# The MLP's second weight: every operand summed, split and stored during the first product, and one load per item in the second

## The chip, the core and the metric

One core of a Trainium2 chip runs the kernel. The metric is device time in microseconds for one execution, lower is better; the time of a kernel is the median of its runs.

## What is computed

The reference is one layer of a decoder: RMSNorm, an input projection whose columns feed four head groups (gated convolution, two attentions with compressed keys or latents, stick-breaking attention), their norms, an output projection and a residual; then the part that matters here, the MLP on x of 2048 x 1024 with 4096 hidden columns, all in float32:

```python
h2 = rms_norm(x, norm2_w[l])
x = x + jnp.square(jax.nn.relu(h2 @ ffn_w1[l])) @ ffn_w2[l]
```

## The kernel before

**Split operands.** A float32 operand goes through the matmul as two parts, `hi` (a copy rounded to the matmul's type) and `lo` (the operand less `hi`), and a product is three matmuls, hi x hi, hi x lo and lo x hi. `split_s` (L216) makes the parts: ScalarE copies (L219), VectorE or GpSimd subtracts (L220).

**Seven products for eight.** Both MLP products are made of 2 x 2 blocks by a Strassen-like scheme: seven products of sums of quarters, `PARTS` (L1689) naming for each product the quarter of the first and of the second operand. `sums` (L1875) turns the first operand's quarters step by step into the sums, on GpSimd (four per chunk, L1878 to L1883).

**First product** (`items1`, 224 items of 12 matmuls, 128x512 each): per slice f of 256 hidden columns and half of the tokens seven items. `load1` fetches a slice of `ffn_w1` on SP's queue into `yr` or `hr`; `prep1` splits a quarter into a slot of `wslot` (L1846), 11 slots cut from the two big tiles `b0` and `b1` (`parts`, seven pieces of 2048 columns) that the attention has left; preparation runs 7 items ahead. `product1` sums into a PSUM bank (six banks in turn), evacuates it by VectorE, or by ScalarE for product 1 (L1920), and `hidden` (L1900) applies relu and square on ScalarE and stores to `ud` in DRAM from ScalarE's queue (L1907). The other operand lies split in SBUF (`form`).

**Sums of the second weight.** `weight_sums` (L2008) runs beside the first product, one step per item: for each chunk it loads the four quarters of `ffn_w2` into `rawb` (L2012), makes four sums on GpSimd (L2017) and stores them unsplit to `wsd` (L2021), all on SP's queue.

**Second product** (`items2`, two halves of the tokens). The 4096 rows of the second weight go in chunks `CH`: one double (two blocks of 128 rows per quarter), one single, six double, and a last single one without the scheme. A chunk has seven items (four for the last), an item four token tiles, each of 6 (double) or 3 (single) matmuls into one bank; `add` (L2113) adds the bank to an accumulator `accp` by VectorE (L2117), or copies it by ScalarE in a half's first chunk (L2115). The last chunk is `plain2` (L2132), two items to a bank. `combine` (L2150) adds accumulators to each other, half on VectorE and half on GpSimd, after the last chunk of the scheme; `store` (L2154) writes the rows out.

`preps2` prepares items ahead of the product, as many as the ring `ops` has pairs (ten tiles, so five). `prep2` (L2025) splits both operands of an item into the item's pair: the first from `ZA` (loaded by `load_a`, L1992, from `ud`), the second from `ZB` (loaded by `load_bs`, L2005, 512 KB from `ffn_w2` or, for the four sums, from `wsd`, into a ring `rb` of eight). `LOA` and `LOB` name the subtracting engine for each of a chunk's seven items:

```python
split_s(za[ka], oa[:, 0, 0:nm], oa[:, 1, 0:nm], eng=E[LOA[j]])
split_s(ZB.pop(n), ob[:, 0, 0:nm], ob[:, 1, 0:nm], eng=E[LOB[j]])
```

**Order of the work.** The framework orders each engine's instructions when the program is built: program order is the priority, and an instruction goes ahead when its operands are ready and its engine is free in the builder's own timeline. On the chip every engine, and every engine's DMA queue, runs that order and waits at its head. So the weight sums, written one step per item over some 170 items, run in the first part of the product.

Of the kernel before, what the change touches and what calls it, by code (L numbers as in the profile page):

```python
# [20 lines left out]
P = 128  # L21
# [27 lines left out]
LOA, LOB = 'ddddddd', 'pdpdddd'  # L49
# [83 lines left out]
def _build(ctx, nc, tc, a, out, dbg, upto):  # L133
# [1544 lines left out]
    def tail():  # L1678
# [17 lines left out]
        with ExitStack() as c1:  # L1696
# [131 lines left out]
            for i in range(NT):  # L1828
# [7 lines left out]
                if i:  # L1836
# [10 lines left out]
                     for (t, c) in [(parts[q], 2) for q in (3, 2, 0, 1, 6)] + [(b0[:, 8192:9216], 1)] for n in range(c)]  # L1847
# [115 lines left out]
            def op2(t):  # L1963
                return t.rearrange("p (s m n) -> p s m n", s=2, m=2)

            ops = [op2(parts[q]) for q in (0, 1, 6, 3, 2)] + [None] + [op2(parts[q]) for q in (4, 5)] + [None, None]
            NOP = len(ops)


            ra, rb = [], []  # L1970
            ZA, ZB = {}, {}
            done2, loaded_b = [0], [0]

            wsd = {(c, p): dram.tile([P, ch[1], 512], F32, name="wsd%d_%d" % (c, p))
                   for c, ch in enumerate(CH) if ch[2] for p in (4, 5, 6, 7)}
# [18 lines left out]
            def load_bs(upto):  # L1994
                while loaded_b[0] < min(upto, len(items2)):
                    k = loaded_b[0]
                    h, c, j = items2[k]
                    nm, inside = CH[c][1:]
                    z = ZB[k] = blocks(rb[k % 8], nm)
                    p = ORDER2[j]  # L2000
                    if inside and p > 3:
                        src = wsd[c, p]
                    else:
                        src = quarter(c, PARTS[p][1] if inside else PLAIN[j][1])
                    Q[W2Q].dma_start(z, src)  # L2005
                    loaded_b[0] += 1

            def weight_sums(c):  # L2008
                nm = CH[c][1]
# [5 lines left out]
                for (n, o, x, y, op, p) in ((0, 22, 22, 12, ALU.subtract, 7), (1, 12, 12, 11, ALU.subtract, 5),  # L2015
                                            (2, 11, 22, 11, ALU.add, 6), (3, 21, 21, 11, ALU.subtract, 4)):
                    E[SUB[n]].tensor_tensor(z[o], z[x], z[y], op)  # L2017
                    yield
                    yield
                for (q, p) in ((22, 7), (12, 5), (11, 6), (21, 4)):  # L2020
                    Q[W2Q].dma_start(wsd[c, p], z[q])  # L2021
                    yield
                    yield
# [77 lines left out]
            with ExitStack() as c2:  # L2101
                wr = c2.enter_context(tc.tile_pool(name="fr", bufs=1, side="right", reuse_waits="tile"))
                wp = c2.enter_context(tc.tile_pool(name="fw", bufs=1, reuse_waits="tile"))
                for n in (5, 8, 9):
                    ops[n] = wr.tile([P, 2, 2, 512], F32R, name="op2_%d" % n)
# [105 lines left out]
```

## Time and profile before

| | us |
|---|---|
| median of three runs | 3069.57 |
| the runs | 3068.2 to 3080.05 |
| the profiled execution | 3078.75 |
| its span (first to last instruction) | 3077.0 |

| engine | busy | share of the span |
|---|---|---|
| TensorE | 2914.2 | 95% |
| VectorE | 2265.1 | 74% |
| ScalarE | 1647.7 | 54% |
| GpSimd | 1337.6 | 43% |

The first product of the MLP begins near 1785 us of the span, the second at 2407.6. The engine names in the rows below: PE is TensorE (PEld its weight loads), DVE VectorE, ACT ScalarE, POOL GpSimd, SP SyncE, and a q behind one is its queue. A row of a timeline has the start, the duration, the engine, the line, the operation, the tiles (written <- read), the form and the count, and in brackets the idle time before it and what ended that.

### The profile page before, as it was taken

To read this page: it belongs to the slowest core of one execution; us is meant where nothing else is said; L and a number is where in the kernel's file an instruction comes from. 1 tells how busy PE (TensorE), PEld (TensorE's weight loads), DVE (VectorE), ACT (ScalarE), POOL (GpSimd) and SP (SyncE) were. 2 spreads that over 40 slices of the span, in tenths; PEclk is the share of its full clock that TensorE was granted. 3 is DMA by queue.
4 is the path that set the end of the run, shared out by engine and by line. 5 is a ranking of instruction groups with operands and counts; after the bars stand their busy time and mean duration, and the time that the engine had idled before them with its cause. 6 is when DMAs were issued, how large, how long until landed. Compare 5 with 4: busy or idle time off the path is not lost. (4 is left out here: it accounts for less than half of the span.)

```text
span 3077.0 us, 43654 instructions
## 1 busy us (share of the span) xinstructions
PE 2914.2 (95%) x14111; PEld 2324.2 (76%) x14123; DVE 2265.1 (74%) x4782; ACT 1647.7 (54%) x3328; POOL 1337.6 (43%) x1311
## 2 busy tenths in 40 slices
PE   7999999899888999999989989999999999989998
PEld 7867898687666667766668868887888777877887
DVE  7843357798777787777678676766444699999998
ACT  5622334677686768787855344456555533334331
POOL 1210102455565667676522267635222343364334
PEclk9999999899888999999999999999999999999999
DMA  8556643522320110010034569745333644364431
GB/s 243 161 137 210 195 146 112 144 81 61 102 83 21 28 37 21 27 41 15 28 118 145 187 209 322 279 144 175 110 109 110 233 151 150 117 215 157 151 127 72
DMA packets 311752, 398.18 MB, mean 129 GB/s; under 512 B 67167, under 2 KB 206091, under 8 KB 311267
## 3 DMA queue, kind: packets, MB, share of 16 engines
q1 hardware_dynamic: 279635, 351.73, 36.1%
q10 hardware_dynamic: 31344, 41.82, 3.7%
q8 instruction: 112, 1.84, 0.2%
q0 software_dynamic: 544, 1.84, 0.2%
q14 instruction: 117, 0.96, 0.1%
HBM read 262.64 MB, written 132.69 MB: 128 GB/s over the span
## 5 line engine op out<-in xcount | busy, mean ns | idle before, releaser
L971 POOL TENSOR_TENSOR pw<-pf,ph 128x512 fp32r<-128x512 f32 (+2 forms) x264 | 326.3, 1248 | 145.3 <-ACT pf L968 101.9
L139 PE MATMUL ptr<-form,big 128*128 128x512 f32 x1152 | 281.0, 393 | 8.6 <-ACT ft L1920 4.5
L139 PE MATMUL pmm<-form,big 128*128 128x512 f32 x1152 | 278.6, 391 | 2.3 <-ACT big L219 1.9
L139 PEld LDWEIGHTS ptr<-form,big 128*128 128x128 f32 x1152 | 216.9, 189 | 57.5 <-ACT ft L1920 5.4
L963 ACT ACTIVATE ph<-pmm 128x512 fp32r<-128x512 f32 (+2 forms) x366 | 210.5, 575 | 93.0 <-PE pmm L139 71.4
L139 PEld LDWEIGHTS pmm<-form,big 128*128 128x128 f32 x1152 | 216.0, 188 | 49.7 <-ACT big L219 2.3
L139 PE MATMUL pmm<-big 128*128 128x512 f32 (+5 forms) x816 | 218.6, 394 | 6.2 <-DVE accp L2117 5.2
L139 PE MATMUL pmm<-whl,hth 128*128 128x256 f32 (+2 forms) x1024 | 218.4, 304 | 4.1 <-ACT hth L219 3.6
L1306 POOL TENSOR_TENSOR sg<-sg,ce 128x512 f32<-128x512 f32 (+3 forms) x160 | 155.6, 974 | 144.3 <-DVE ce L1304 116.8
L219 ACT ACTIVATE big<-raw 128x1024 fp32r<-128x1024 f32 (+2 forms) x116 | 100.8, 882 | 178.2 <-PE ptr L139 97.9
L220 DVE TENSOR_TENSOR big<-hr,big 128x512 fp32r<-128x512 f32 (+1 forms) x125 | 141.6, 1135 | 64.5 <-ACT big L219 64.1
L139 PE MATMUL pmm<-big,big 128*128 128x512 f32 (+5 forms) x672 | 178.7, 393 | 10.6 <-DVE accp L2117 10.0
L139 PEld LDWEIGHTS pmm<-big 128*128 128x128 f32 (+2 forms) x816 | 154.3, 192 | 42.2 <-ACT op L219 5.7
L139 PE MATMUL ptr<-big 128*128 128x512 f32 (+2 forms) x645 | 178.9, 400 | 4.3 <-DVE mx L1208 1.7
L139 PE MATMUL pmm<-big,ar 128*128 128x512 f32 x736 | 182.3, 397 | 0.0
L139 PEld LDWEIGHTS pmm<-whl,hth 128*128 128x128 f32 x1024 | 169.8, 195 | 10.6 <-issue 4.6
L220 DVE TENSOR_TENSOR big<-yr,big 128x512 fp32r<-128x512 f32 (+1 forms) x125 | 126.2, 1012 | 54.7 <-ACT big L219 53.9
L139 PE MATMUL pmm<-hth,whl 128*128 128x512 f32 x480 | 157.1, 403 | 7.7 <-ACT whl L223 4.5
L139 PEld LDWEIGHTS pmm<-big,ar 128*128 128x128 f32 x736 | 136.7, 189 | 29.0 <-ACT ar L219 0.3
L2117 DVE TENSOR_TENSOR accp<-accp,ptr 128x512 f32<-128x512 f32 x224 | 151.6, 677 | 6.7 <-PE ptr L139 6.4
L139 PEld LDWEIGHTS pmm<-big,big 128*128 128x128 f32 (+2 forms) x672 | 125.1, 190 | 41.1 <-DVE accp L2117 11.9
L2117 DVE TENSOR_TENSOR accp<-accp,pmm 128x512 f32<-128x512 f32 x224 | 151.5, 676 | 6.3 <-PE pmm L139 6.3
(488 smaller groups left out, 7961.6 us busy)
## 6 DMA issues: line engine op xcount, KB each, us to landing
ud<-ft ACTq DMA_DIRECT2D x124, 256.0 KB, 2.0
xt<-x SPq DMA_DIRECT2D x32, 512.0 KB, 6.0
yr<-ffn_w SPq DMA_DIRECT2D x16, 1024.0 KB, 6.0
hr<-ffn_w SPq DMA_DIRECT2D x16, 1024.0 KB, 5.2
rawb<-ffn_w SPq DMA_DIRECT2D x28, 512.0 KB, 4.9
wsd<-rawb SPq DMA_DIRECT2D x28, 512.0 KB, 6.2
rawb<-ud SPq DMA_DIRECT2D x28, 512.0 KB, 3.3
raw<-wsd SPq DMA_DIRECT2D x28, 512.0 KB, 6.2
```

The costliest lines, as they stand in the source:

```text
L139: anchor[0] = pe.matmul(o, l, r, start=start, stop=stop)
L219: act.activation(hi, src, AF.Copy)
L220: (eng or dve).tensor_tensor(lo, src, hi.bitcast(F32), ALU.subtract)
L963: act.activation(ph[:, 0:n], pl[:, 0:n], AF.Exp)
L971: sub.tensor_tensor(pw[:, 0:n], pf[:, 0:n], ph[:, 0:n].bitcast(F32), ALU.subtract)
L1306: pool.tensor_tensor(sg[:, o:512], sg[:, o:512], ce[:, o + 1:513], ALU.mult)
L2117: dve.tensor_tensor(acc[p][:, t], acc[p][:, t], pt, ALU.add)
```

## The change

The second operand of the second product is prepared whole beside the first product. `weight_forms` takes the place of `weight_sums`: for all nine chunks it loads the four quarters, and for each of the seven operands of a chunk (the last chunk: its four quarters) `two_parts` splits it (ScalarE copies, VectorE subtracts) and, a step later, stores both parts to `wsd` from ScalarE's queue. `hi` goes to one of two halves of `parts[6]`; `lo` to the other half where the quarter is still needed for sums, otherwise over the quarter itself. The four sums per chunk stay on GpSimd. In the second product `prep2` splits only the first operand; the second comes as both parts in one load on SP's queue, straight into its place in the ring. `load_bs`, `rb`, `ZB` and `LOB` go; the ring grows from ten tiles to twelve (six items ahead) and takes its pieces of the big tiles in another order; `wslot` has nine slots, since `parts[6]` is now the staging.

```diff
-                     for (t, c) in [(parts[q], 2) for q in (3, 2, 0, 1, 6)] + [(b0[:, 8192:9216], 1)] for n in range(c)]
+                     for (t, c) in [(parts[q], 2) for q in (3, 2, 0, 1)] + [(b0[:, 8192:9216], 1)] for n in range(c)]
...
-            ops = [op2(parts[q]) for q in (0, 1, 6, 3, 2)] + [None] + [op2(parts[q]) for q in (4, 5)] + [None, None]
+            ops = [op2(parts[q]) for q in (3, 6, 0, 2, 1)] + [None] + [op2(parts[q]) for q in (4, 5)] + [None] * 4
...
-            wsd = {(c, p): dram.tile([P, ch[1], 512], F32, name="wsd%d_%d" % (c, p))
-                   for c, ch in enumerate(CH) if ch[2] for p in (4, 5, 6, 7)}
+            wsd = {(c, p): dram.tile([P, 2, ch[1], 512], F32, name="wsd%d_%d" % (c, p))
+                   for c, ch in enumerate(CH) for p in (range(1, 8) if ch[2] else (11, 12, 21, 22))}
+            stage = [parts[6][:, n * 1024:(n + 1) * 1024] for n in range(2)]
+            staged_n = [0]
...
-            def weight_sums(c):
-                nm = CH[c][1]
+            def weight_forms(c):
+                nm, inside = CH[c][1:]
                 z = {q: blocks(ra[n], nm) for n, q in enumerate((22, 12, 11, 21))}
                 for q in z:
                     Q[W2Q].dma_start(z[q], quarter(c, q))
                 for _ in range(5):
                     yield
...
+                def two_parts(q, p, keep):
+                    staged_n[0] += 1
+                    hi = blocks(stage[staged_n[0] % 2], nm)
+                    lo = blocks(stage[(staged_n[0] + 1) % 2], nm) if keep else z[q].bitcast(F32R)
+                    split_s(z[q], hi, lo)
+                    yield
+                    act.dma_start(wsd[c, p][:, 0], hi.bitcast(F32))
+                    act.dma_start(wsd[c, p][:, 1], lo.bitcast(F32))
...
+                if inside:
+                    yield from two_parts(22, 3, True)
+                    add(0, 22, 22, 12, ALU.subtract)
+                    yield
+                    yield
+                    yield from two_parts(11, 1, True)
+                    add(1, 12, 12, 11, ALU.subtract)
+                    add(2, 11, 22, 11, ALU.add)
+                    yield
+                    yield
+                    yield from two_parts(21, 2, True)
+                    add(3, 21, 21, 11, ALU.subtract)
                     yield
                     yield
                 for (q, p) in ((22, 7), (12, 5), (11, 6), (21, 4)):
-                    Q[W2Q].dma_start(wsd[c, p], z[q])
-                    yield
+                    yield from two_parts(q, p if inside else q, False)
                     yield
...
-                split_s(ZB.pop(n), ob[:, 0, 0:nm], ob[:, 1, 0:nm], eng=E[LOB[j]])
+                Q[W2Q].dma_start(ob[:, :, 0:nm].bitcast(F32), wsd[c, p if inside else kb])
...
-                    load_bs(min(done2[0] + 8, len(rb) if len(rb) < 8 else len(items2)))
...
-            wsums = iter([g for c, ch in enumerate(CH) if ch[2] for g in [weight_sums(c)]])
+            wsums = iter([weight_forms(c) for c in range(len(CH))])
...
-                    load_bs(4)
...
-                for n in (5, 8, 9):
+                for n in (5, 8, 9, 10, 11):
```

## Rows read from the trace of the kernel before

**Rows 1.** The page, part 1: busy us, share of the span, instructions.

```profile
PE 2914.2 (95%) x14111; PEld 2324.2 (76%) x14123; DVE 2265.1 (74%) x4782; ACT 1647.7 (54%) x3328; POOL 1337.6 (43%) x1311
```

**Rows 2.** Stretches: length, then PE, PEld, DVE, ACT, POOL busy; clock, DMA, GB/s.

```profile
1785.00:2413.00 628.00, 614.86 (x2664) 501.54 (x2665) 374.81 (x463) 327.70 (x545) 293.23 (x183) 0.99 0.52 181
1830.00:1980.00 150.00, 149.81 (x655) 122.66 (x654) 106.29 (x103) 69.75 (x119) 116.64 (x60) 1.00 0.88 312
2413.00:3073.00 660.00, 630.89 (x2690) 508.11 (x2688) 627.06 (x678) 233.10 (x266) 283.96 (x126) 0.98 0.44 152
```

**Rows 3.** Timeline of PE in the second product.

```profile
2407.63 1.52 PE L139 MATMUL pmm<-big 128*128 128x512 f32 x6
...
2452.30 0.84 PE L139 MATMUL pmm<-big 128*128 128x512 f32 x3
...
2460.51 0.87 PE L139 MATMUL pmm<-big,big 128*128 128x512 f32 x3
...
2471.72 1.62 PE L139 MATMUL pmm<-big 128*128 128x512 f32 x3 [2.43 <-DVE accp L2117]
...
2476.92 1.55 PE L139 MATMUL pmm<-op,op 128*128 128x512 f32 x6
...
2548.90 1.52 PE L139 MATMUL pmm<-op,big 128*128 128x512 f32 x6
...
2588.85 1.53 PE L139 MATMUL pmm<-op,op 128*128 128x512 f32 x6
...
2717.97 0.84 PE L139 MATMUL pmm<-op,op 128*128 128x512 f32 x3
...
2733.75 0.86 PE L139 MATMUL pmm<-big 128*128 128x512 f32 x3
...
3050.53 0.84 PE L139 MATMUL pmm<-op,op 128*128 128x512 f32 x3
...
3061.47 0.86 PE L139 MATMUL pmm<-big 128*128 128x512 f32 x3
...
3072.01 0.86 PE L139 MATMUL ptr<-op,big 128*128 128x512 f32 x3
```

**Rows 4.** Waits of PE, 2416 to 3077: us in total, times, longest us.

```profile
PE pmm L139 <- DVE accp L2117: 15.2, 5, 6.7
PE ptr L139 <- DVE accp L2117: 12.5, 10, 2.6
```

**Rows 5.** Timeline of all engines, 2464 to 2468.

```profile
2464.22 2.37 POOL L1879 TENSOR_TENSOR rawb<-rawb,rawb 128x1024 f32<-128x1024 f32 x1
2464.32 3.35 DVE L220 TENSOR_TENSOR big<-rawb,big 128x1024 fp32r<-128x1024 f32 x1
...
```

**Rows 6.** Instructions on two tiles, op and accp: ns min/median/max, first and last start.

```profile
L219 ACT ACTIVATE op<-hr x12: 614/1044/1051, 2400.5 to 3012.4; 128x1024 fp32r<-128x1024 f32 x10, 128x512 fp32r<-128x512 f32 x2
L220 DVE TENSOR_TENSOR op<-raw,op x28: 678/1214/3421, 2422.4 to 3043.8; 128x1024 fp32r<-128x1024 f32 x23, 128x512 fp32r<-128x512 f32 x5
L220 POOL TENSOR_TENSOR op<-raw,op x8: 1293/2408/3400, 2425.5 to 2986.2; 128x1024 fp32r<-128x1024 f32 x6, 128x512 fp32r<-128x512 f32 x2
...
L2117 DVE TENSOR_TENSOR accp<-accp,ptr x224: 672/675/690, 2421.8 to 3072.9; 128x512 f32<-128x512 f32 x112
```

**Rows 7.** A stretch at the start of the second product, columns as in rows 2.

```profile
2410.00:2420.00 10.00, 9.54 (x42) 7.48 (x41) 3.48 (x2) 5.87 (x10) 2.47 (x2) 1.00 1.04 395
```

**Rows 8.** The page, part 6: DMA issues, KB each, median us to landing.

```profile
wsd<-rawb SPq DMA_DIRECT2D x28, 512.0 KB, 6.2
...
accp<-x2d SPq DMA_DIRECT2D x8, 1024.0 KB, 6.5
```

**Rows 9.** Issues on the tile ud from ScalarE's queue: ns min/median/max.

```profile
L1907 ACTq DMA_DIRECT2D ud<-ft x124: 325/326/359, 1824.4 to 2418.1; - x124
```

**Rows 10.** Waits of SP's queue, 1790 to 2413: us in total, times, longest.

```profile
SPq L2021 <- POOL rawb L2017: 63.8, 25, 6.8
SPq L2012 <- DMA wsd<-rawb: 38.6, 16, 4.9
```

More of the change, by code (lines that the diff above doesn't have):

```diff
@@ L48 @@
 SU1, SUA, SUB = 'pppp', 'pppp', 'pppp'
-LOA, LOB = 'ddddddd', 'pdpdddd'
+LOA = 'ddddddd'
 SQE = 'aaaa'
@@ L1964, in op2 @@
                 return t.rearrange("p (s m n) -> p s m n", s=2, m=2)
-            ops = [op2(parts[q]) for q in (0, 1, 6, 3, 2)] + [None] + [op2(parts[q]) for q in (4, 5)] + [None, None]
+            ops = [op2(parts[q]) for q in (3, 6, 0, 2, 1)] + [None] + [op2(parts[q]) for q in (4, 5)] + [None] * 4
             NOP = len(ops)
-            ra, rb = [], []
-            ZA, ZB = {}, {}
-            done2, loaded_b = [0], [0]
-            wsd = {(c, p): dram.tile([P, ch[1], 512], F32, name="wsd%d_%d" % (c, p))
-                   for c, ch in enumerate(CH) if ch[2] for p in (4, 5, 6, 7)}
+            ra, ZA = [], {}
+            done2 = [0]
+            wsd = {(c, p): dram.tile([P, 2, ch[1], 512], F32, name="wsd%d_%d" % (c, p))
+                   for c, ch in enumerate(CH) for p in (range(1, 8) if ch[2] else (11, 12, 21, 22))}
+            stage = [parts[6][:, n * 1024:(n + 1) * 1024] for n in range(2)]
+            staged_n = [0]
             def blocks(t, nm):
@@ L1992, in load_a @@
                 Q[UQ].dma_start(z, src if nm == 2 else src[:, m % 2:m % 2 + 1])
[L1994 to L2006, printed above, removed]
-            def weight_sums(c):
-                nm = CH[c][1]
+            def weight_forms(c):
+                nm, inside = CH[c][1:]
                 z = {q: blocks(ra[n], nm) for n, q in enumerate((22, 12, 11, 21))}
@@ L2014, in weight_sums, with add @@
                     yield
-                for (n, o, x, y, op, p) in ((0, 22, 22, 12, ALU.subtract, 7), (1, 12, 12, 11, ALU.subtract, 5),
-                                            (2, 11, 22, 11, ALU.add, 6), (3, 21, 21, 11, ALU.subtract, 4)):
-                    E[SUB[n]].tensor_tensor(z[o], z[x], z[y], op)
+                def two_parts(q, p, keep):
[6 more added lines that the diff above has]
+                    act.dma_start(wsd[c, p][:, 1], lo.bitcast(F32))
+                def add(n, o, x, y, op):
+                    E[SUB[n]].tensor_tensor(z[o], z[x], z[y], op)
+                if inside:
[10 more added lines that the diff above has]
+                    add(3, 21, 21, 11, ALU.subtract)
                     yield
@@ L2072, in tail @@
             ra += [fb.tile([P, D], F32, name="rawb%d" % n) for n in range(4)]
-            rb += [t[:, n * D:(n + 1) * D] for t in (yr, hr) for n in range(2)]
-            wsums = iter([g for c, ch in enumerate(CH) if ch[2] for g in [weight_sums(c)]])
+            wsums = iter([weight_forms(c) for c in range(len(CH))])
             job = [next(wsums)]
@@ L2103, in tail @@
                 wp = c2.enter_context(tc.tile_pool(name="fw", bufs=1, reuse_waits="tile"))
-                for n in (5, 8, 9):
+                for n in (5, 8, 9, 10, 11):
                     ops[n] = wr.tile([P, 2, 2, 512], F32R, name="op2_%d" % n)
-                more = [wr.tile([P, D], F32, name="raw2_%d" % n) for n in range(8)]
-                ra += more[0:4]
-                rb += more[4:8]
+                ra += [wr.tile([P, D], F32, name="raw2_%d" % n) for n in range(4)]
                 acc = {p: (wr if n < 3 else wp).tile([P, NT4, 512], F32, name="accp%d" % p)
```

## The prediction

> **What bounds the kernel now.** First the page's busy shares: TensorE 95%, VectorE 74% [rows 1]. An average over the whole span says nothing of one stage, so I cut the MLP into stretches [rows 2]. In the first product's 628 us TensorE is busy 614.9, VectorE 375, ScalarE 328. Even where today's weight sums run (1830 to 1980: GpSimd busy 117 of 150 us, DMA share 0.88) it is busy 149.8. That product is bound by its matmuls and has room on every other engine. In the second product VectorE is busy 627 of 660 us: there two engines stand at their limit.
>
> What that costs is read from TensorE's timeline [rows 3]. Undisturbed, twelve groups of three matmuls take 8.21 us (2452.30 to 2460.51), 0.684 each. The second product has 2712 matmuls: per half seven double chunks of 7 x 24, one single chunk of 7 x 12, and 16 x 6 at the end. That is 904 groups, 618 us. It runs from 2407.63 to 3072.9 (the last group, at 3072.01, takes 0.86): 665 us, so **47 us are lost**. Where:
> - After the single chunk, ten groups take 16.41 us (2460.51 to 2476.92) instead of 6.84: 9.6 lost, part of it waiting and part in slow matmuls (the group at 2471.72 waits 2.43 us and takes 1.62). The same happens in the second half: 19 together.
> - At the end of the first half seven groups take 15.78 us (2717.97 to 2733.75) instead of 4.79, and at the end of the second 10.94 (3050.53 to 3061.47): 11 and 6 lost, while the accumulators are added up.
> - In a settled double chunk 168 matmuls take 39.95 us (2548.90 to 2588.85) instead of 38.3: 1.65 lost. That and the first items make up the other 11.
>
> The waits name the cause: TensorE's 27.7 us of idle time there are nearly all for a VectorE evacuation [rows 4], that is, for a PSUM bank. VectorE is late because of its splits. While GpSimd ran a 2.37 us sum, one split took 3.35 us [rows 5]; the median is 1.21, the longest 3.42, while an evacuation is always 0.67 to 0.69 [rows 6]. So a GpSimd operation that meets a split adds about 2.1 us to it.
>
> **The change, part by part.**
>
> *Second operand no longer split in the second product.* Of 120 items 98 are double and 22 single. ScalarE loses 120 copies: 98 x 1.044 + 22 x 0.614 = 116 us, off the path. VectorE loses the splits marked d, 70 double and 14 single: 70 x 1.21 + 14 x 0.68 = 95 us unhindered. GpSimd loses 28 double and 8 single: 28 x 2.41 + 8 x 1.29 = 78 us [rows 6]. VectorE falls from 627 to at most 532 of 660.
>
> Per double chunk VectorE now has 28 x 0.675 + 12 x 1.21 = 33.4 us unhindered, and six GpSimd operations (two splits, four sums) that can add 2.1 each: 46 at most. The measured 39.95 [rows 3] means that about half of them hit. After it, 18.9 + 7 x 1.21 = 27.4, plus 2.1 for half of the four sums: 32, under TensorE's 38.3. Gain there: 8 of the 11. The Trainium skill (SBUF — State Buffer, "Who interferes with whom") says that a VectorE operation with two SBUF inputs and a GpSimd operation that reads SBUF exclude each other for a whole instruction. By that rule all four sums would hit, 36 us, still under 38.3; the trace agrees with blocking as such (3.35 beside 2.37).
>
> At the single chunk TensorE needs 19.2 us for seven items, VectorE 18.9 for evacuations plus the splits of the double chunk ahead: today 12 x 1.21 + up to 6 x 2.1, 46 in all, 27 too much, of which 9.6 shows; so lookahead and the six banks cover about 17. Then: 18.9 + 8.5 + half of 8.4 = 31.6, 12 too much, covered. I take 8 of 9.6, twice: 16. At the ends of the halves the accumulators' additions stay, on both engines; of the 17 lost there I take 4. **Sum of the gain: 28 us**, between 11 (only VectorE's freed time in settled chunks) and 47 (all of it).
>
> *Loads.* An item's load grows from 512 KB to 1 MB, both parts, straight into the ring. Settled: 1 MB plus a share of the first operand's 2 MB per chunk in 5.5 us is about 235 GB/s, under the 395 that the trace shows at its fullest [rows 7]. One such load lands in about 6.5 us (a 1 MB accumulator load [rows 8]), and the ring gives it five items, 27 us. It now waits in SP's queue for TensorE to leave the slot, with the next chunk's first operands, the residual loads and half the output stores behind it; those too are issued items ahead. At the start of each half the engines are full already (share 1.04 at 2410 [rows 7]); seven items' extra 0.5 MB at 395 GB/s is 9 us more. Bounds 0 and 18; I take 3, since this product's queue runs ahead of TensorE.
>
> *The new forms beside the first product.* 60 operands, 49 double and 11 single: ScalarE 58 us of copies, VectorE 67 unhindered (182 if each took the longest), 120 store issues at 0.326 [rows 9], 39 us; GpSimd's 32 sums stay; four loads more; SP loses 32 stores. ScalarE: 328 busy [rows 2], 40 of issuing 124 ud stores, and these 97: 465 of 628. VectorE: 375 + 67 to 182, at most 557. Both stay under TensorE. Stores grow from 15 to 54.5 MB, over a longer stretch than today's 15.
>
> Pace: two staging halves. A kept operand fills both, so the next waits for copy, split, two stores and their landing (6.2 us for 512 KB [rows 8]), some 9 us; the others alternate, some 5. A double chunk is 3 x 9 + 4 x 5 plus loads and the last landing, 57 us; all nine about 450, from 1815 to 2265, before the first operands are due some 20 us ahead of 2407. ScalarE waits in its queue for VectorE's half and for the staging; behind stand its evacuation of product 1, relu and square, and the copies for TensorE's weights. Cover: six banks of 2.7 us and nine slots (eleven before) with seven items of lookahead. No row has such waits on ScalarE; bounds 0 (covered) and 42 us (below). I take 2, nearest to the 149.8 of 150 where SP's own waits reached 4.9 [rows 2, 10].
>
> **Sum:** 28 - 3 - 2 = 23 us off. The profiled execution took 3078.75 us for a span of 3077.0; less 23, 3055.75. It lies 9.2 above the median of the runs, 3069.57, so **3047 us**.
>
> **The rivals.**
>
> *ScalarE becomes the first product's bound (slower).* Every second store stands in ScalarE's queue until VectorE has the low part: 1.21 to 3.42 us [rows 6], 60 times 73 to 205 us. On 465 that is 538 to 670, against 628: at most 42 over, which is 3089. It decides from 163 us of waiting, 2.7 per operand; a staging wait counts too. For it: SP stood 63.8 us in 25 waits for GpSimd's sums before stores, and 38.6 in 16, up to 4.9, for stores to land [rows 10]. Against: ScalarE can do other work first where the stores are emitted one item after the split. The Trainium skill (DMA: Bandwidth & Descriptors, "Anatomy of one DMA") says that the DMA engines never wait on semaphores, the issuing sequencer does. By that rule these waits fall on ScalarE as reckoned; rows 10 show it on SP. Chance 0.21.
>
> *The sums alone keep the stalls (no difference).* GpSimd's four sums per chunk remain, and a run of them could still hold VectorE after the single chunk: without those 16 us, 3063. For it: sums of 2.37 to 3.37 us stand back to back there. Against: two of that run's operations go. Chance 0.12.
>
> *Late loads at the starts (no difference).* If the 18 us show, 15 more than I took: 3062. For: share 1.04. Against: the queue is ahead elsewhere. Chance 0.11.
>
> That all forms are really made ahead is plain from the diff: I see no case in which it does not do what it says.
>
> **How the numbers follow.** My forecast has 0.56. About 0.5% (15 us, to 3054) is what a measurement here can tell from no change; the forecast's own range, 3038 to 3056, lies nearly all on the faster side: 0.50 of its 0.56. The remaining 0.06 and the two middle rivals give 0.29 for the same; the slower side gets the 0.21 of the ScalarE case. The range reaches down to 3036 (gain 34, nothing given back) and up to 3085, through the two middle rivals and the milder part of the ScalarE case; outside lie about 0.15 above and 0.05 below.
>
> **What would show it.** Right: in the second product VectorE below 540 busy, the ten groups after the single chunk under 9 us, the settled chunk at 38.3 to 38.6, waits for evacuations under 15 us; the first product ends as far after its start as before. Wrong: TensorE in the first product waiting for ScalarE copies or evacuations; TensorE in the second waiting for a load into the ring; forms still being stored after 2380; a settled chunk still near 40.

## The result and the profile after

Four runs gave a median of 3102.06 us (3099.97 to 3104.59), against 3071.22 for the kernel before in the same comparison: a ratio of 1.0095, 95% interval 1.0080 to 1.0109. **The change costs 31 us**; 3047 was forecast, and the range ended at 3085. The profiled execution's span is 3102.8 us.

Busy us, share of the span and instructions of each engine, from the page of the changed kernel:

```profile
PE 2914.1 (94%) x14111; PEld 2325.1 (75%) x14123; DVE 2176.0 (70%) x4758; ACT 1594.3 (51%) x3268; POOL 1243.3 (40%) x1275
```

VectorE, ScalarE and GpSimd all have less to do than in [rows 1], and the kernel is slower. Busy shares do not tell where. Two stretches do, the two products, and between them the one on which the forecast rested (length, then PE, PEld, DVE, ACT, POOL busy; clock, DMA share, GB/s):

```profile
1785.00:2470.00 685.00, 628.59 (x2653) 506.35 (x2653) 444.29 (x521) 378.02 (x602) 293.64 (x181) 0.96 0.64 227
1830.00:1980.00 150.00, 149.22 (x653) 121.86 (x651) 109.45 (x124) 87.80 (x137) 73.51 (x43) 1.00 0.77 276
2470.00:3098.00 628.00, 617.57 (x2687) 505.80 (x2686) 466.57 (x594) 130.33 (x149) 189.78 (x92) 0.99 0.68 251
```

The second product begins at 2464.49 instead of 2407.63: **57 us lost in the first product**. From there to the end of its last group it takes 634.4 us instead of 665.2: **31 us won in the second**. Part of the 57 is thus paid back, and 26 us of the span stay lost. In 1830 to 1980 TensorE is busy 149.2, practically the 149.8 of [rows 2]: the loss is not there.

TensorE's timeline of the second product:

```profile
2464.49 1.55 PE L139 MATMUL pmm<-big,big 128*128 128x512 f32 x6
...
2515.20 0.84 PE L139 MATMUL pmm<-op,op 128*128 128x512 f32 x3
...
2523.82 1.61 PE L139 MATMUL pmm<-op,big 128*128 128x512 f32 x6
...
2552.22 1.08 PE L139 MATMUL pmm<-big 128*128 128x512 f32 x4
...
2590.50 0.84 PE L139 MATMUL pmm<-op,big 128*128 128x512 f32 x3
...
2762.22 0.85 PE L139 MATMUL ptr<-big,op 128*128 128x512 f32 x3
2769.14 1.65 PE L139 MATMUL pmm<-op,op 128*128 128x512 f32 x3 [6.06 <-DVE accp L2122]
...
2774.42 1.00 PE L139 MATMUL pmm<-op,op 128*128 128x512 f32 x2
...
3097.35 1.56 PE L139 MATMUL ptr<-op,big 128*128 128x512 f32 x6
```

Read it against [rows 3]. The last ten groups of the single chunk, 2515.20 to 2523.82, take 8.62 us instead of 16.41. A settled double chunk, 2552.22 to 2590.50, takes 38.28 instead of 39.95. What is left of the stalls is one wait at the seam of the halves: five groups take 12.20 us from 2762.22, 8.8 too much. The second half's end has none. TensorE's waits for evacuations there (us in total, times, longest), 27.7 in [rows 4]:

```profile
PE pmm L139 <- DVE accp L2122: 8.4, 4, 6.1
PE ptr L139 <- DVE accp L2122: 1.9, 1, 1.9
```

Now the first product in slices of 100 us, columns as above:

```profile
1900.00:2000.00 100.00, 96.67 (x420) 78.08 (x420) 73.81 (x81) 59.08 (x91) 50.87 (x28) 1.00 0.81 292
2000.00:2100.00 100.00, 93.26 (x401) 74.25 (x400) 78.50 (x81) 58.22 (x91) 49.82 (x28) 1.00 0.82 300
2100.00:2200.00 100.00, 62.01 (x203) 45.82 (x202) 70.67 (x69) 55.36 (x89) 56.83 (x32) 0.74 0.84 300
2200.00:2300.00 100.00, 100.00 (x441) 82.47 (x440) 54.39 (x78) 53.90 (x89) 32.78 (x24) 1.00 0.48 164
```

Two of these slices in the kernel before:

```profile
2000.00:2100.00 100.00, 100.00 (x440) 82.27 (x439) 63.52 (x85) 59.61 (x103) 44.51 (x32) 1.00 0.48 161
2100.00:2200.00 100.00, 97.24 (x418) 78.77 (x417) 54.91 (x79) 56.83 (x96) 35.69 (x27) 0.98 0.39 132
```

In the slice 2200 to 2300 nothing is lost: 441 matmuls. Measured by that, the slice 2100 to 2200 lacks 238, 54 us of matmuls; the same slice before lacked 23. Of the 54 TensorE is idle for 38; the other 16 or so are slower matmuls, at a granted clock of 0.74 on average against 1.00 in the slices around it. The two slices ahead of it lack 21 and 40 (5 and 1 before), so some 12 us are lost ahead of it. What stands in the slice 2100 to 2200 is the placing: while the last two slices of hidden columns of the first half run, `place` copies and splits the second half's 28 token tiles (24 into `form`, four into a piece of the big tiles) as soon as TensorE has left the places, and TensorE needs the first of them a few items later. What TensorE waited for there, four largest:

```profile
PE ptr L139 <- ACT form L219: 13.7, 2, 7.2
PE pmm L139 <- ACT form L219: 11.4, 3, 4.6
PE pmm L139 <- POOL form L220: 7.8, 2, 5.1
PE ptr L139 <- DVE form L220: 3.5, 1, 3.5
```

None of these waits is there before beyond 0.4 us. Some of ScalarE's work in the placing, from the first token copy to the last (the fourth row is relu), and GpSimd's sums in the same stretch (busy, mean ns, idle time before and its releasers):

```profile
L219 ACT ACTIVATE form<-fst 128x512 fp32r<-128x512 f32 x24 | 14.5, 622 | 6.4 <-DMA fst<-h2f 1.7 <-issue 1.6 <-DMA rawb<-ffn_w 1.0
L219 ACT ACTIVATE big<-rawb 128x1024 fp32r<-128x1024 f32 x12 | 12.6, 1048 | 11.9 <-DMA wsd<-big 8.3 <-DVE rawb L220 2.6 <-DMA rawb<-ffn_w 0.9
L219 ACT ACTIVATE big<-yr 128x512 fp32r<-128x512 f32 x12 | 7.3, 624 | 12.6 <-DMA yr<-ffn_w 6.1 <-PE ptr L139 2.8 <-POOL yr L1879 2.5
...
L1902 ACT ACTIVATE ft<-ft 128x512 f32<-128x512 f32 x11 | 6.8, 621 | 8.6 <-DVE ft L1923 4.6 <-DVE ft L1935 3.3 <-DVE ft L1939 0.7
...
L2015 POOL TENSOR_TENSOR rawb<-rawb,rawb 128x1024 f32<-128x1024 f32 x8 | 20.6, 2572 | 14.0 <-DVE big L220 11.5 <-issue 2.5
```

The 24 copies into `form` are the same as before, but twelve copies of the second weight's operands stand among them, and eight sums among GpSimd's half of the token splits. Before, none did: the last sum was done by 1972, and the placing ran from 2063 to 2120. Now the forms' stores go on to 2206 and the placing runs from 2084 to 2181. How one of the twelve holds a token copy:

```profile
2177.19 1.06 ACT L219 ACTIVATE big<-rawb 128x1024 fp32r<-128x1024 f32 x1 [2.45 <-DMA wsd<-big]
...
2178.68 0.61 ACT L219 ACTIVATE form<-fst 128x512 fp32r<-128x512 f32 x1
...
2179.72 1.04 ACT L219 ACTIVATE big<-rawb 128x1024 fp32r<-128x1024 f32 x1
...
2180.66 0.61 ACT L219 ACTIVATE form<-fst 128x512 fp32r<-128x512 f32 x1
...
2181.33 1.22 PE L139 MATMUL pmm<-form,big 128*128 128x512 f32 x2 [4.27 <-ACT form L219]
```

ScalarE waits 2.45 us at the head of its queue for a store to land and free the staging; behind that copy, and another such copy, stand the two token copies, and TensorE has waited 4.27 us for the second. Transfers have slowed down as well (KB each, median us to landing; before 4.9 and 3.0):

```profile
rawb<-ffn_w SPq DMA_DIRECT2D x28, 512.0 KB, 11.9
...
fst<-h2f SPq DMA_DIRECT2D x36, 256.0 KB, 6.0
```

### The profile page after: what moved, and what is told of

Its sections match the earlier page's. It is cut to its first block, busy times and chain, and to the rows that moved or that the text cites. A ratio compares the mean times of both kernels' runs of the same rounds, so it can differ in the third digit from the quotient of the medians.

```text
span 3102.8 us, 43582 instructions
## 1 busy us (share of the span) xinstructions
PE 2914.1 (94%) x14111; PEld 2325.1 (75%) x14123; DVE 2176.0 (70%) x4758; ACT 1594.3 (51%) x3268; POOL 1243.3 (40%) x1275
## 5 line engine op out<-in xcount | busy, mean ns | idle before, releaser
L139 PE MATMUL ptr<-form,big 128*128 128x512 f32 x1152 | 288.4, 400 | 28.4 <-ACT form L219 13.7
L139 PE MATMUL pmm<-form,big 128*128 128x512 f32 x1152 | 285.3, 398 | 25.6 <-ACT form L219 12.9
L2122 DVE TENSOR_TENSOR accp<-accp,ptr 128x512 f32<-128x512 f32 x224 | 152.4, 683 | 56.7 <-PE ptr L139 54.6
L219 ACT ACTIVATE big<-rawb 128x1024 fp32r<-128x1024 f32 (+1 forms) x100 | 97.9, 979 | 173.9 <-PE ptr L139 121.1
L139 PE MATMUL pmm<-big 128*128 128x512 f32 (+4 forms) x672 | 178.5, 391 | 0.9 <-DVE ce L1304 0.8
L139 PE MATMUL pmm<-whl,htl 128*128 128x256 f32 (+2 forms) x512 | 152.4, 299 | 1.2 <-DVE htl L220 1.2
L968 ACT ACTIVATE pf<-pmm 128x512 f32<-128x512 f32 (+2 forms) x264 | 152.2, 576 | 0.8 <-DVE mx L1208 0.8
L139 PEld LDWEIGHTS pmm<-big 128*128 128x128 f32 (+2 forms) x672 | 126.0, 191 | 29.7 <-DVE ce L1304 1.8
L220 DVE TENSOR_TENSOR big<-hr,big 128x512 fp32r<-128x512 f32 x112 | 112.0, 1004 | 49.6 <-ACT big L219 49.5
## 6 DMA issues: line engine op xcount, KB each, us to landing
rawb<-ffn_w SPq DMA_DIRECT2D x28, 512.0 KB, 11.9
```

Of the source, the lines that this page charges most:

```text
L139: anchor[0] = pe.matmul(o, l, r, start=start, stop=stop)
L219: act.activation(hi, src, AF.Copy)
L220: (eng or dve).tensor_tensor(lo, src, hi.bitcast(F32), ALU.subtract)
L968: act.activation(pf[:, 0:n], pl[:, 0:n], AF.Exp)
L2122: dve.tensor_tensor(acc[p][:, t], acc[p][:, t], pt, ALU.add)
```

## Where the loss comes from: collision with the placing, or the work itself

Four theories stood against each other: ScalarE's stores and waits, as in the slower rival; the token fetches standing behind the chunk loads in SP's queue; the added work as such, wherever it runs; or its meeting the placing.

**Six chunks' forms left out.** Only chunks 0, 1 and the last are formed; the six other double chunks read chunk 0's operands, so the work of these six is left out.

```diff
...
-            wsums = iter([weight_forms(c) for c in range(len(CH))])
+            wsums = iter([weight_forms(c) for c in (0, 1, len(CH) - 1)])
```

> The changed kernel with forms made of three chunks alone (the first double one, the single one, the last); the other six double chunks read the first one's forms, so six ninths of the second weight's rows are left out of the result, while the second product's loads and matmuls stay as they are. All forms are then made before about 1930, long before the placing. Theory A: the first product ends where it did before (2405 to 2412) and the second keeps its gain of 31 us: 3036 to 3046. If the second product's gain hangs on the first product being late (more done ahead), it would shrink: 3050 to 3070. Theory B asks for the same as A here.

3044.56 us, ratio 0.9902 (0.9886 to 0.9919); the first product ends at 2406.15. Its slice 2100 to 2200:

```profile
2100.00:2200.00 100.00, 95.80 (x410) 77.42 (x409) 53.68 (x78) 56.74 (x95) 37.45 (x28) 0.98 0.43 141
```

The whole loss is for the six chunks' forms. The second product, which loads as much as ever, keeps its gain, and TensorE waits for no load in it, here or in the changed kernel.

**Held back until the placing is over.** From one chunk on, no load is issued before the last token tile is placed (one-column copies that read the last form and write into the loads' four buffers make the order certain).

```diff
...
+                if c == GATE:
+                    while not placed:
+                        yield
+                    for n in range(4):
+                        dve.tensor_copy(ra[n][:, 0:1], bf[3][:, 1, 3, 511:512].bitcast(F32))
                 for q in z:
...
```

From chunk 6:

> The changed kernel, but the loads of its last three chunks of weight forms (6, 7 and 8) wait until the token forms of the second half have all been placed, by four one-column copies from the last placed form into the four raw tiles. Theory A (the weight forms' instructions stand in the in-order queues of ScalarE, VectorE, GpSimd and SP ahead of the placing, and TensorE starves for forms between 2095 and 2181 in the changed kernel): those 45 to 50 us come back, 3050 to 3060 us. Theory B (ScalarE's waits for its own stores and for the staging cost wherever the forms run): the same waits come later, 3085 to 3105. Theory C (only SP's queue, whose loads wait for stores to land): comes back too, as under A.

From chunk 5:

> As the kernel with the gate at chunk 6, with one chunk more behind the gate (5 to 8). Theory A: as good, 3047 to 3060; a few us better if chunk 5 (its loads were issued 2026 to 2044) still ran into the placing, and a few worse only if the four late chunks are not stored when the second product needs the raw tiles near 2380. Theory B: 3085 to 3105.

3066.14 us (0.9982, 0.9970 to 0.9993) and 3063.68 (0.9970, 0.9958 to 0.9981). All work is there; only its place moved, and 36 and 38 us come back, as the theory of the collision foretold; both times lie a little above its ranges, which ended at 3060. Two slices with the gate at chunk 5, the second with the forms running again:

```profile
2100.00:2200.00 100.00, 91.03 (x385) 73.02 (x383) 67.07 (x80) 58.45 (x94) 55.12 (x32) 0.97 0.75 266
2200.00:2300.00 100.00, 94.94 (x403) 76.04 (x404) 71.41 (x87) 60.04 (x96) 42.60 (x25) 0.98 0.87 314
```

In the second, beside ordinary items, the full forms cost TensorE 5 of 100 us. In the first, with the last part of the placing and the gate's release, 9 are lost, where the changed kernel lost 38. So most of the cost is the meeting with the placing. Some loss stays: with the gate at chunk 5 the first product ends at 2418.89, 11 us later than before.

**The queue theories.** Stores from SP instead of ScalarE (both `act.dma_start` become `sync.dma_start`):

> The changed kernel with the 120 stores of the weight forms issued from SP's queue again instead of ScalarE's. Theory B (ScalarE's queue is the trouble): ScalarE no longer stops for the low parts, most of the 57 us lost in the first product come back, 3045 to 3065. Theory A: the copies that wait for the staging stay on ScalarE and the sums on GpSimd, so the placing still starves: 3085 to 3110. Theory C (SP's queue): SP now waits for the low parts as well, ahead of the fetches: slower than the change, 3105 to 3150.

Token fetches from GpSimd's queue instead of SP's (`HRQ` from `'sync'` to `'pool'`):

> The changed kernel with the fetches of the stored token forms (36 of 256 KB, 28 of them at the placing) issued from GpSimd's queue instead of SP's. Theory C (the fetches stand in SP's queue behind weight loads that wait up to 22.7 us for stores to land): 40 us or more come back, 3050 to 3065. Theory A: the fetch was not what was late most often; the splits of the fetched forms on ScalarE and GpSimd still stand behind weight forms: 3085 to 3105, or slower by GpSimd's own issuing.

3092.73 us (1.0062, 1.0047 to 1.0077) and 3115.81 (1.0138, 1.0123 to 1.0153). The first with its slice 2100 to 2200, the second with its fetches' landing:

```profile
2100.00:2200.00 100.00, 66.78 (x235) 50.49 (x234) 74.99 (x76) 57.04 (x92) 58.23 (x31) 0.78 0.90 319
```

```profile
fst<-h2f POOLq DMA_DIRECT2D x36, 256.0 KB, 5.6
```

Nine us come back with the stores, and in that slice TensorE still has 235 matmuls of 441. The fetches are no better off on another queue: the kernel is 14 us slower than the changed one. From 2080 to 2185 of the changed kernel weight loads at the head of SP's queue waited 24.5 us for stores to land, and the fetches themselves 27.7 us for VectorE to split the tile whose place they take; on GpSimd's queue they no longer stand behind the loads, and nothing is won. They land in 5.6 us there and in 6.0 on SP. The Trainium skill (DMA: Bandwidth & Descriptors, "Issuing engines are not separate DMA queues") says that DMAs of all issuing engines interleave on the same 16 DMA engines, and that issuing from several of them saves only the time that the issuing takes; the landing times agree.

**Two controls on the kernel before.** Nine `wslot` slots instead of eleven, the ring as it was (the last four items of the first product then read other operands, a part left uncomputed), and all of the second operand's splits on VectorE:

```diff
-                     for (t, c) in [(parts[q], 2) for q in (3, 2, 0, 1, 6)] + [(b0[:, 8192:9216], 1)] for n in range(c)]
+                     for (t, c) in [(parts[q], 2) for q in (3, 2, 0, 1)] + [(b0[:, 8192:9216], 1)] for n in range(c)]
...
-LOA, LOB = 'ddddddd', 'pdpdddd'
+LOA, LOB = 'ddddddd', 'ddddddd'
```

> The kernel before, with nine slots for the first product's split weights instead of eleven, as in the change. If the nine slots cover seven items of lookahead, no difference: 3066 to 3076. If the change's losses in the first product came in part from fewer slots: 3080 or more.

> The kernel before, with the second operand's splits all on VectorE (two of a chunk's seven leave GpSimd). If the second product's loss came of VectorE's own load, 28 double splits more (34 us) make it worse: 3085 to 3110. If GpSimd's blocking of VectorE's splits was the larger part (each hit 2.1 us), the two nearly cancel: 3065 to 3080.

3067.12 us (0.9975, 0.9965 to 0.9984): the two slots cost nothing. And 3079.18 (1.0012, 1.0000 to 1.0025). The second product there, columns as in [rows 2]:

```profile
2413.00:3073.00 660.00, 629.90 (x2682) 508.37 (x2681) 628.31 (x712) 232.11 (x265) 205.13 (x91) 0.98 0.46 151
```

VectorE has 34 instructions more than in [rows 2] and is busy just as long. So the splits that GpSimd made had cost VectorE about as much in blocking as they saved it, and moving them from one engine to the other wins nothing. The change takes them out of both, and VectorE is busy 467 of 628 us.

## Which part of the forms holds the placing

If one resource were short, leaving out what uses it should bring the loss back. Five kernels, each the changed one with a single part less or a single place more.

**Four staging halves** (a second piece, `parts[1]`; seven `wslot` slots, and the ring's pieces in the order 3, 6, 1, 2, 0):

```diff
...
-            stage = [parts[6][:, n * 1024:(n + 1) * 1024] for n in range(2)]
+            stage = [parts[q][:, n * 1024:(n + 1) * 1024] for q in (6, 1) for n in range(2)]
...
```

> The changed kernel with four staging halves instead of two (a second piece of the big tiles; the first product's ring then has seven slots instead of nine, the second product's ring takes its pieces in another order). Stores stay in ScalarE's queue, nothing is held back. Theory S, ScalarE's copies wait at the head of its queue for the staging halves (24.4 us in 17 waits for stores to land) and hold the placing of the second half's token forms: those waits go, at least half of the 57 us comes back, the first product ends at or before 2435 and the time is 3050 to 3075. Theory Q, any late load or store beside the placing holds some engine's queue, GpSimd's and VectorE's too, and the staging is only one of several holds: 5 to 20 us come back, as with the stores on SP, the first product ends at 2445 to 2460 and the time is 3082 to 3097. If seven slots are too few for the first product, TensorE waits for the first weight's copies and the time is above 3102.

3101.67 us (1.0107, 1.0089 to 1.0125): nothing comes back, less than either theory expected, though staging is the wait that ScalarE's rows show most: 16 weight copies stand in the placing here. That the seven slots ate up a gain is not excluded by this run. Two kernels below, both with seven slots, speak against it: with four staging halves and the work held back the ratio is the same as with two and nine slots, and with seven token tiles most of the loss returns.

**No sums, no loads, no stores, no splits.** Without the four sums per chunk (`add` does nothing), the loads, the stores, or the copies and subtractions, the last three for six chunks:

```diff
-                    E[SUB[n]].tensor_tensor(z[o], z[x], z[y], op)
+                    pass
...
-                for q in z:
+                for q in z if c in (0, 1, len(CH) - 1) else ():
...
+                    if same[c] == c:
                         act.dma_start(wsd[c, p][:, 0], hi.bitcast(F32))
...
+                    if c in (0, 1, len(CH) - 1):
                         split_s(z[q], hi, lo)
...
```

> The changed kernel without the four sums of quarters per chunk on GpSimd in the second weight's forms (the operands that should be sums are then plain quarters, so the four products of each chunk that need them are left wrong: that part of the computation is left out). Loads, copies, splits and stores stay as they are. Theory G, the sums wait on GpSimd for late loads and stores and hold GpSimd's half of the token forms' splits behind them: the first product ends at or before 2435 and the time is 3050 to 3075. Theory Q, each of the queues of ScalarE, VectorE and GpSimd is held by the weight forms' waits for loads and stores, and the sums are one of several holds: 0 to 20 us come back, the first product ends at 2445 to 2465, the time is 3080 to 3102. In both, TensorE's waits for GpSimd's share of the forms fall below the 7.8 us of the changed kernel.

> The changed kernel without the loads of the quarters for six of the seven double chunks (their sums, splits and stores run on what the first chunk left in the buffers, so these six chunks' operands are wrong: that part of the computation is left out). Theory L, the loads land late (11.9 us against 4.9 before) and the sums and copies that need them wait at the head of the queues: at least half of the 57 us returns, the first product ends at or before 2435, 3045 to 3075. Theory D, the DMA engines are full beside the placing and what is late is the token fetches: the loads are a quarter of the added bytes, 10 to 20 us return, 3082 to 3092. Theory E, the copies, subtractions and sums themselves take the engines' time: under 10 us, 3092 to 3105.

> The changed kernel without the stores of six of the seven double chunks (the second product reads the first chunk's operands for them, so these six chunks' share of the result is left wrong: that part of the computation is left out). Loads, copies, subtractions and sums stay. Theory D, full DMA engines: the stores are three quarters of the added bytes, at least 40 us return, the first product ends at or before 2425, 3044 to 3062. Theory L, late loads: the loads land sooner without the stores beside them, 25 to 45 us return, 3055 to 3077. Theory E, the engines' own work: under 15 us (what ScalarE spends on issuing and waiting), 3087 to 3105.

> The changed kernel without the copies and the subtractions of the second weight's operands for six of the seven double chunks (what the staging and the quarters hold is stored as it is, so these six chunks' operands are wrong: that part of the computation is left out). Loads, sums and stores stay, in the same bytes. Theory E, the engines' own work, or the copies and subtractions standing at the heads of ScalarE's and VectorE's queues: at least half of the 57 us returns, the first product ends at or before 2435, 3045 to 3075. Theory D, full DMA engines: under 12 us, 3090 to 3105. Theory L, late loads met by the sums on GpSimd: 5 to 20 us, 3082 to 3097.

3082.20 us (1.0030, 1.0019 to 1.0042), 3102.86 (1.0093, 1.0075 to 1.0111), 3090.24 (1.0064, 1.0041 to 1.0087) and 3118.26 (1.0144, 1.0125 to 1.0163). No part alone returns more than 20 us. The first lies where many small holds put it, the next two where the engines' own work does, and the last is off every range. Two traces show that the loss moves. Without the stores, which pace the forms, the last of those that stay is out at 2074, before the placing begins, which then takes its usual 56 us; but VectorE and GpSimd got their work in a shorter time, and the loss is spread over 1900 to 2200 (342, 348 and 387 matmuls). The first and the last of these slices:

```profile
1900.00:2000.00 100.00, 85.54 (x342) 66.22 (x340) 98.76 (x78) 60.02 (x88) 75.04 (x32) 0.95 0.48 158
2100.00:2200.00 100.00, 90.73 (x387) 72.96 (x386) 63.44 (x85) 62.75 (x110) 42.61 (x31) 0.97 0.54 172
```

In the first VectorE is busy 98.8 of 100 us. Without the splits, nothing holds the stores apart (the last is issued at 2128.6 instead of 2206), the DMA engines are full and the operands of the first product itself come late: TensorE is busy 47 of 100 us.

```profile
1900.00:2000.00 100.00, 46.98 (x172) 36.11 (x171) 22.36 (x32) 21.76 (x36) 21.40 (x13) 0.73 1.00 392
```

The waits of 1880 to 2000 in that kernel name the way it goes (us in total, times, longest): ScalarE for a store to land, TensorE's weights for ScalarE, an evacuation once for 36 us:

```profile
ACT big L219 <- DMA wsd<-big: 39.1, 5, 24.5
PEld pmm L139 <- ACT big L219: 36.8, 1, 36.8
PE pmm L139 <- DVE ft L1932: 36.4, 1, 36.4
```

**What the runs have in common.** Read from ScalarE's timeline of each: when the copies of token tiles into `form` ran (24 or 25 of them), and how many copies of the second weight's operands stand among them:

| kernel | token copies, us | length | weight copies among them |
|---|---|---|---|
| before | 2063.4 to 2120.3 | 56.9 | 0 |
| after | 2083.7 to 2181.3 | 97.5 | 12 |
| six chunks left out | 2061.3 to 2118.0 | 56.7 | 0 |
| held back from chunk 5 | 2064.7 to 2121.9 | 57.2 | 0 |
| stores from SP | 2077.3 to 2170.4 | 93.1 | 12 |
| fetches from GpSimd | 2085.2 to 2191.4 | 106.2 | 14 |
| four staging halves | 2078.4 to 2187.2 | 108.8 | 16 |
| no sums | 2060.6 to 2151.0 | 90.4 | 12 |
| no loads | 2088.6 to 2176.9 | 88.3 | 12 |
| no stores | 2107.3 to 2163.6 | 56.2 | 0 |

The placing takes 56 to 57 us wherever no weight copy stands in it, and 88 to 109 where 12 to 16 do. In the changed kernel it is 40.6 us longer. By ScalarE's rows the twelve weight copies themselves take 24.5 of that, 12.6 busy and 11.9 waiting at the head of the queue; ScalarE also stood 12.6 us before copies of the first weight (2.4 before), half of it for late loads, and 8.6 before relu for VectorE (2.4 before). The engine's order is fixed when the program is built, so a weight copy that waits, for a store, a load or a sum, holds the token copies behind it, whichever it waits for. That fits with no part alone being to blame, but it is read from the table: no run changed the order alone. The length alone does not order the times either: without loads the placing takes 88.3 us and the first product ends at 2464.06, without sums 90.4 and 2432.64. The kernel without splits has no weight copies to count there; its placing, after its last store, 2135.6 to 2192.9, takes 57.2 as well.

## Giving the placing more room

What is left is the other side: the placing has three token tiles in flight, `NHR` = 3, so each fetch waits for the split of the tile three before it, and each copy for its fetch. Seven in flight for the second half, four of them in `parts[1]` (slots and ring as with four staging halves):

```diff
...
+                    if h and k % 7 >= NHR:
+                        fetched[q] = more_f[k % 7 - NHR]
+                    else:
                         fetched[q] = kr.tile([P, 4, P], F32, name="fst", tag="fst", bufs=NHR)
...
-                fetch(h, k + NHR)
+                fetch(h, k + (7 if h else NHR))
...
```

In the changed kernel, and as a control in the kernel before:

> The changed kernel with seven token tiles fetched ahead for the second half instead of three (four of them in a piece of the big tiles; the first product's ring then has seven slots). Theory F, the ring of three fetches at a doubled landing time sets the pace of the placing: the placing keeps up with TensorE, at least 30 of the 57 us return, the first product ends at or before 2435 and the time is 3047 to 3073. Theory Q, the placing's copies and splits stand in order behind the weight forms' on ScalarE, VectorE and GpSimd: at most 12 us return, 3088 to 3105.

> The kernel before with seven token tiles fetched ahead for the second half instead of three (nine slots in the first product's ring, the second product's ring takes its pieces in another order). Theory F, three fetches are enough at a landing time of 3.0 us and too few at 6.0: the kernel before has only the 2.8 us to win that TensorE loses beside its placing, 3066 to 3075. If the deeper ring is a gain in itself: 3030 to 3060.

3060.75 us (0.9956, 0.9939 to 0.9972), the first product ending at 2424.14, and 3063.97 (0.9966, 0.9956 to 0.9977), ending at 2400.54. So 40 of the 57 us of the first product return; the kernel before wins 7 there as well, between the 2.8 that the ring alone was to give it and a gain in itself. Three slices of the changed kernel with seven, then of the kernel before with seven:

```profile
1900.00:2000.00 100.00, 95.11 (x408) 76.93 (x407) 77.16 (x81) 57.24 (x89) 52.22 (x28) 0.98 0.82 298
2000.00:2100.00 100.00, 91.79 (x386) 72.44 (x385) 80.60 (x83) 61.36 (x98) 59.20 (x33) 0.98 0.82 301
2100.00:2200.00 100.00, 87.58 (x371) 70.11 (x370) 81.25 (x87) 64.32 (x105) 64.13 (x35) 0.97 0.78 277
```

```profile
1900.00:2000.00 100.00, 98.98 (x433) 80.89 (x432) 69.16 (x73) 46.83 (x80) 66.47 (x35) 1.00 0.77 268
2000.00:2100.00 100.00, 100.00 (x439) 82.06 (x438) 65.28 (x85) 60.89 (x107) 46.65 (x32) 1.00 0.50 161
2100.00:2200.00 100.00, 100.00 (x438) 82.03 (x437) 54.51 (x80) 56.43 (x96) 35.16 (x26) 1.00 0.39 127
```

The slice at 0.74 of the clock is gone. What stays, 24 us against the control, is spread over all three slices. The weight copies among the token copies are now 3, the line in the placing (2079 to 2133):

```profile
L219 ACT ACTIVATE big<-rawb 128x1024 fp32r<-128x1024 f32 x3 | 3.1, 1046 | 1.3 <-DMA fst<-h2f 1.3
```

So the deeper ring did two things at once: tiles come earlier on the chip, and the builder, which sees copies ready earlier, puts them ahead of the weight copies. The table speaks for the order as the larger part, without proving it. Against the landing as the direct cause speaks the first of ScalarE's rows in the placing, above: of the 6.4 us that its token copies stood idle there, 1.7 were for a fetch (13.0 of 13.3 in the kernel before, where no weight copies stand between). The two were not tried apart: that would need seven tiles in flight in the order built for three.

With seven in flight and the stores from SP as well:

> The changed kernel with seven token tiles fetched ahead and the stores of the forms from SP's queue instead of ScalarE's, nothing held back. If the rest of the loss is ScalarE's issuing and waiting for the low parts: about 10 us below the kernel with seven fetches alone, 3045 to 3054. If it is the forms' own copies, subtractions and sums: 3056 to 3064.

3062.65 us (0.9970, 0.9960 to 0.9981): no gain, so the stores' place in ScalarE's queue is not what is left. The theory that remains is the forms' own copies, subtractions and sums among ordinary items; no run takes these apart.

**Put together.** Held back from chunk 5, with stores from SP; then with four staging halves; then, instead of these, with seven token tiles in flight:

> The gate at chunk 5, and the 120 stores of the forms from SP's queue. With the collision at the placing gone, what is left of the first product's loss is 11 us. If ScalarE's stops for the low parts make it (theory B for the rest): 3050 to 3057. If it is the evacuations on VectorE and ScalarE behind the forms' own copies and splits: 3058 to 3068. If SP's queue then holds up the weight loads of the first product: 3068 or more.

> The faster version of the earlier runs (chunks from the sixth on held back until the second half's token forms are placed, stores from SP's queue) with four staging halves as well, and the first product's ring at seven slots. Theory S: the rest of what that version loses in the first product, some 9 us, is for the staging, and goes: 3042 to 3049. Theory Q: the rest is for evacuations and copies that ScalarE and VectorE do late for the added work itself, and stays: 3050 to 3056. Seven slots too few: above 3058.

> The faster version (chunks from the sixth on held back until the second half's token forms are placed, stores from SP's queue) with seven token tiles fetched ahead instead of three and seven slots in the first product's ring. Theory F: what is left of the loss at the placing, some 5 us, goes: 3043 to 3049. Theory Q: no more than the version with four staging halves: 3048 to 3056.

3053.22 us (0.9931, 0.9917 to 0.9946), 3049.64 (0.9933, 0.9916 to 0.9951) and 3044.44 (0.9910, 0.9887 to 0.9933). The staging halves change nothing in the ratio, and leave open which theory holds there (3049.64 lies between the two ranges). **The last is 0.9% faster than the kernel before**: its first product ends at 2404.05, 3.6 earlier than before, and its second product keeps the change's gain. Part of this is the deeper ring, which the kernel before can have too: with it that kernel stands at 0.9966, so what the held-back change adds to it is about 0.6%. Its first product still ends 3.5 us later than that kernel's (2400.54).

```profile
2000.00:2100.00 100.00, 98.01 (x426) 79.12 (x425) 76.25 (x88) 63.85 (x110) 52.33 (x34) 1.00 0.64 219
2100.00:2200.00 100.00, 94.46 (x405) 74.81 (x404) 82.44 (x91) 60.58 (x96) 52.99 (x30) 1.00 0.83 303
```

## Why the prediction was wrong

- **The second operand out of the second product: right.** 31 us were won; 28, less 3 for loads, were forecast. VectorE is busy 467 of 628 us (under 540 was the mark), the ten groups that the prediction has after the single chunk, which are its last ten, take 8.62 (under 9), a settled chunk 38.28 (38.3 to 38.6), waits for evacuations 10.3 (under 15). At the ends of the halves 8 of the 17 went, not 4. That half of GpSimd's operations hit a split agrees with the control that moved the splits. One reading was loose: the 39.95 us of a settled chunk were not the rule, since 1.65 lost in each of the twelve settled double chunks would be 20 us, and the prediction's own sum had 11 left for them.
- **Loads: as forecast, little or nothing.** No wait of TensorE in the second product is for a load; the runs can't tell the 3 us taken for them from none.
- **The forms beside the first product: the step that failed.** The term was "I take 2, nearest to the 149.8 of 150", between 0 and 42; it measured 57. The row was read right and taken from the wrong place. The stretch 1830 to 1980 had the weight sums beside ordinary items, and even the new forms cost 0.6 us there. But by the prediction's own pace they would run from 1815 to 2265 (they ran from 1807 to 2206), and so for the first time beside the placing of 2063 to 2120, a stage that the prediction never looked at. Its cover was reckoned in PSUM banks and weight slots, which hold for the weights; the token tiles have three places and are needed within items of being free.
- **The upper bound failed with it.** The 42 us counted what ScalarE might have to do or wait, 670 us against the product's 628. ScalarE was busy 378 of 685, and 55 of 100 in the slice where most was lost. Here the queue did not have to be full to stop TensorE: the placing took 97.5 us instead of 57, with ScalarE idle for part of that time.
- **The slower rival: right in direction, not in mechanism.** Waits fell on ScalarE, as rows 10 foretold for SP, and TensorE waited for ScalarE copies. But moving the stores off ScalarE gave back 9 us, and moving them when the ring was deeper gave nothing, while moving the forms away from the placing gave back 36 and 38: what counts is where they run against the placing, not ScalarE's load.
- **The other rivals fell.** The sums alone did not keep the stalls, and there were no late loads at the starts.

## What to carry to other kernels

When work is moved beside a stage, find every stage that it will now overlap, at its new length, and cost it at the tightest: the one whose data is used soonest after it is made. The queues here run in a fixed order, so the price of hoisted work includes the waits that it puts ahead of urgent instructions, and the engine's idle share did not bound it. Either keep background work out of that stage, or give the stage's own ring more places, and look at the order that is built, not only at the times.

## What the runs showed that was not expected

Leaving work out made the kernel slower: without the copies and subtractions by 16 us. By the trace those had spaced the stores; unspaced, the DMA share was 1.00 over 100 us and TensorE stood 36.4 us on one evacuation. And four more places in a ring of three, which do no work, were worth more (40 us) than any single part of the added work.
